# Down projection in seven products: the first two operands of each next product are fetched and split before the evictions, and product 0's first two use the weight pool

## The chip, the cores and the metric

The kernel runs on one core of a Trainium2 chip. The metric is the device time of one execution in microseconds; the number given for a kernel is the median of several executions. The core has five engines that each work through an instruction stream of their own, in order: TensorE (PE in the profile, with its weight loads as PEld), VectorE (DVE), ScalarE (ACT), GpSimd (POOL) and SyncE (SP). SyncE, GpSimd and, for a few stores, ScalarE issue the DMA transfers; an instruction that waits holds up all that stand behind it on its engine.

## The reference

Two layers over 1024 latent tokens and 256 context tokens of width 1024, all in float32: layer 0 mixes with Fourier groups and a Hyena convolution, layer 1 with neighbourhood attention. Each ends with a SwiGLU feed-forward block of width 2816. That block's last product is what the change touches:

```python
def swiglu(u, w_gate, w_up, w_down):
    return (jax.nn.silu(u @ w_gate) * (u @ w_up)) @ w_down
...
        h_lat = h_lat + g1 * y_lat
        h_lat = h_lat + g2 * swiglu(modulate(rms_norm(h_lat, norm2_g[i]), sh2, sc2),
                                    ffn_w_gate[i], ffn_w_up[i], ffn_w_down[i])
        if not last:
            ...
            h_ctx = h_ctx + cg2 * swiglu(modulate(rms_norm(h_ctx, norm2_g[i]), csh2, csc2),
                                         ffn_w_gate[i], ffn_w_up[i], ffn_w_down[i])
    return rms_norm(h_lat, final_g)
```

`h_lat` is the latent stream, `h_ctx` the context stream; the context is carried through layer 0 only.

## The kernel before

Float32 precision is built from pairs: every operand is split into a rounded high half and the rest, and a product is three matmuls (high x high, high x low, low x high). `split` (L284 to L288) does it: ScalarE casts the high half (L286), VectorE subtracts it from the source (L288). Large latent products are computed by the Strassen-Winograd scheme: seven products of half-size blocks instead of eight.

**Gate and up.** `ffn` (L1309) runs eleven blocks of gate and up. Each block's weights come through the pool `pw` (two buffers for each of the tags `ws`, `wh`, `wl`): raw weights in `ws`, their halves in `wh` and `wl` and in smaller tiles. The matmuls are at L1264; ScalarE copies a running accumulator out before TensorE goes on adding to it (`snap`, L1269). VectorE combines the hidden block (L1357 to L1363), and GpSimd stores seven combinations of it to DRAM (`bops`). Between the blocks, four sums of the down weights are formed for later and stored (`sops`).

**Down.** `down` (L1414) computes the seven products p = 0 to 6 over 1024 tokens. Each has eleven steps i (`n2`). A step takes one operand pair: `operands` (L1420) loads half a tile of weights and half a tile of hidden values on SyncE (L267) and splits the 1024 columns in one go. Its three tiles come from `S4`, the pool `p4` with 20 buffers of 4 KB a partition; the raw data has a tile of its own where the weights come straight from the input (products 0, 1 and 6, `own`), else it lies in the later low half's tile. Then `prods` (L1428) issues 4 x 3 matmuls of 128x512 (L1433), one accumulator for each of four row blocks. The two accumulator sets alternate from product to product.

After the eleven steps `evict` (L1449) adds the four accumulators, scaled, to the residual stream with one VectorE instruction each (L1454). Where a block of the output is complete, ScalarE squares it (L467) for the coming norm, VectorE adds the squares (L472), and in layer 0 ScalarE stores it. The norm itself (L485 to L517) runs in pieces: `hook(i)` (L1472) advances it at fixed steps of the products 6 and later. In the last product a few last steps are held back and done one accumulator after the other.

In layer 0 the products also carry side work: each odd step advances `todo`, which loads and sums the modulation weights (`in_ada_w`, L446 to L453). After product 6 follows the context stream: 22 steps (L1518), each with a 512 KB weight load through `ws` (or a tile of `p4`), its split into `wh` and `wl`, and 24 matmuls of 128x256 (L1536).

**What sets the order.** The program is traced in the order of the Python code, and a scheduler then orders the instructions of each engine by a simulated timeline. A load is traced where it is written but goes out as early as its buffer and its place in SyncE's order allow, so product p + 1's first operands can be loaded during product p. `follow(ins)` (L225) puts the instructions of its block behind `ins` where they run on the same engine. In this program TensorE's matmuls are held in order that way (`end`); the splits and evictions on VectorE and ScalarE are not.

Of the kernel before, what the change touches and what calls it, by code (L numbers as in the profile page):

```python
# [10 lines left out]
F32 = mybir.dt.float32  # L11
# [7 lines left out]
P = 128  # L19
# [181 lines left out]
class Builder:  # L201
# [1212 lines left out]
    def down(self, l, bops, sops, hidc, hs, h, todo, after, keep):  # L1414
        nc, a = self.nc, self.a
        w = a["down"][l]
        n2 = NFB // 2
        self.banks = 6

        def operands(asrc, bsrc, own):  # L1420
            hi, lo = self.S4(F32R), self.S4(F32R)
            f = self.S4() if own else lo.bitcast(F32)
            self.ld(f[:, :512], asrc)
            self.ld(f[:, 512:], bsrc)
            self.split(f, hi, lo)
            return hi, lo

        def prods(acc, ops, j, c0, c1, first, last):  # L1428
            hi, lo = ops
            sl = slice(j * P, (j + 1) * P)  # L1430
            xs = slice(512 + c0, 512 + c1)
            for k, (x, y) in enumerate(((hi, hi), (hi, lo), (lo, hi))):
                m = nc.tensor.matmul(acc[j][:, c0:c1], x[:, sl], y[:, xs], start=first and k == 0, stop=last and k == 2,  # L1433
                                     skip_group_check=True)
            return m.ins

        def load_h(nbs, pc):
            for nb in nbs:
                if pc < 2 or nb % 2 == 0:
                    t = self.S2()  # L1440
                    if pc < 2:
                        self.ldr(t, hs[nb][:, pc * 512:pc * 512 + 512])
                        h.put(0, nb, pc, t)
                    else:
                        for k in (0, 1):
                            self.ldr(t[:, k * 256:k * 256 + 256], hs[nb + k][:, 1024:])
                            h.put(0, nb + k, 2, t[:, k * 256:k * 256 + 256])

        def evict(acc, r, j, pc, final):  # L1449
            nb = 4 * r + j  # L1450
            n = WID[pc]
            c0 = OFF[pc] % 512 if pc > 2 else 0
            t = h.ap(0, nb, pc)
            nc.vector.scalar_tensor_tensor(t, acc[j][:, c0:c0 + n], self.ada_col(l, pc, 5, nb), t, op0=MUL, op1=ADD)  # L1454
            if final and pc < 3:
                self.square(t, nb, pc)
                if l == 0 and pc < 2:
                    self.lda(keep[nb][:, pc * 512:pc * 512 + 512], t)
            elif final and j < 3:
                x = self.TK()  # L1460
                nc.scalar.activation(x[:, :n], t, AF.Square)
                sq = self.sq[1][0][:, c0:c0 + n]
                nc.vector.tensor_tensor(sq, sq, x[:, :n], ADD)

        end = None
        sets = [[self.PP() for _ in range(4)], [self.PP(), self.PP(), self.PQ(), self.PQ()]]
        seq = (("A11", "B11", 0, 1, False), ("A12", "B21", 0, 1, True), ("S2", "T2", 0, 0, False), ("S1", "T1", 1, 0, False),
               ("S3", "T3", 1, 0, True), ("S4", "B22", 0, 0, True), ("A22", "T4", 1, 1, True))
        raw = {"A11": (0, 0), "A12": (1, 0), "A22": (1, 1)}
        done = iter(())  # L1470

        def hook(i):  # L1472
            if i in (3, 6) or i > 7 and l == 0:
                next(done, None)

        for p, (ak, bk, r, pc, final) in enumerate(seq):
            acc = sets[p % 2]
            late = []
            for i in range(n2):
                hook(i)  # L1480
                if p == 0 and i == 6:
                    load_h(range(4), 1)
                if p == 1 and i in (1, 4, 7):
                    load_h(*((range(4), 0), (range(4, 8), 0), (range(4, 8), 1))[i // 3])
                if ak in raw:
                    k, q = raw[ak]
                    src = w[2 * i + k, q]
                else:
                    src = sops[i][ak]
                ops = operands(src, bops[i][bk], ak in raw)  # L1490
                if p == 6 and i >= n2 - (4 if l else 3):
                    late.append((i, ops))
                else:
                    with self.follow(end):
                        for j in range(4):
                            m = prods(acc, ops, j, 0, 512, p in (0, 1, 3) and i == 0, i == n2 - 1)
                    end = m
                if p < 5 and i % 2 or p == 5 and i < 2:
                    next(todo, None)
            for q in (3, 4) if l == 1 and p == 6 else (pc,):  # L1500
                for j in range(4):
                    c0 = OFF.get(q, 0) % 512 if q > 2 else 0
                    for i, ops in late:
                        prods(acc, ops, j, c0, c0 + WID[q], False, i == n2 - 1)
                    evict(acc, r, j, q, final)
                    if q == 3:
                        next(done, None)
                if q > 2:
                    for _ in after(q):
                        pass  # L1510
            if p == 5:
                done = after(0)
        if l == 0:
            for _ in done:
                pass
            done = after(1)
            acc = [self.PP() for _ in range(4)]
            for kb in range(NFB):  # L1518
                hook(kb)
                if kb in (4, 8, 12, 16):  # L1520
                    load_h((kb // 2 - 2, kb // 2 - 1), 2)
                t = self.S2(F32R)
                f = t[:, 256:].bitcast(F32)
                with self.follow(self.last_ldr):
                    self.ldr(f, hidc[kb // 2][:, kb % 2])
                self.split(f, t[:, :256], t[:, 256:])
                f = self.pw.tile([P, 1024], F32, tag="ws", name=self.nm("ws")) if kb % 3 < 2 else self.S4()
                wh, wl = self.pair1()
                self.ld(f.rearrange("p (r k) -> p r k", r=2), w[kb].rearrange("r p k -> p r k"))
                self.split(f, wh, wl)  # L1530
                for nb in range(KB):

                    o = acc[nb // 2][:, nb % 2 * 256:nb % 2 * 256 + 256]
                    with self.follow(end):
                        for k, (x, c) in enumerate(((wh, 0), (wh, 256), (wl, 0))):
                            m = nc.tensor.matmul(o, x[:, nb * P:(nb + 1) * P], t[:, c:c + 256],  # L1536
                                                 start=kb == 0 and k == 0 and nb % 2 == 0,
                                                 stop=kb == NFB - 1 and k == 2, skip_group_check=True)
                    end = m.ins
            for nb in range(KB):  # L1540
                x = h.ap(0, nb, 2)
                nc.vector.scalar_tensor_tensor(x, acc[nb // 2][:, nb % 2 * 256:nb % 2 * 256 + 256],
                                               self.ada_col(0, 2, 5, nb), x, op0=MUL, op1=ADD)
                self.square(x, nb, 2)
            self.last, self.end = after(2), end
        self.banks = 8
# [630 lines left out]
```

## Time and profile before

| | |
|---|---|
| median of 3 executions | 3042.79 us (3039.41 to 3048.79) |
| profiled execution | 3045.79 us, of it span 3044.0 us |
| mean granted TensorE clock | 0.985 |
| layer 0: start of product 0 / product 1 on / context product ends | about 1377 / 1430 / 1690 us |
| layer 1: start of product 0 / products 1 to 6 | about 2788 / 2842 to 3028 us |

How to read the rows below. In the timeline a row has the start in us from the span's start, the duration, the engine, the line, the operation, `written<-read` by tile names, and the number of instructions merged; a bracket gives the idle time before it and the engine, tile and line that ended it. `ps` and `pq` are accumulators, `s` a tile of `p4` (or of the smaller pool `p2`), `ws`, `wh`, `wl` the weight pool, `d` a DRAM buffer, `g` and `tk` tiles of the hidden block. SPq is a load issued on SyncE. In the list of waits a row says who waited for whom: total us, times, longest. In the table by windows each engine has its busy time and, in brackets, its instructions; the last three columns are the granted TensorE clock, the busy share of the DMA engines, and GB/s.

### The profile page before, as it was taken

The numbers are of one execution on the slowest core, as the hardware profiler recorded it, in microseconds if no ns is written. First come the engines' busy times: TensorE is split into PE (matmuls) and PEld (weight loads), VectorE is DVE, ScalarE is ACT, GpSimd is POOL, SyncE is SP. The second block draws the span as 40 slices with busy tenths as digits, with TensorE's granted clock in tenths as the row PEclk, the third lists the DMA queues.
The fourth block names the chain that finished last, engine by engine and source line by source line (L and its number), as shares of the span: only waits on it lengthen the run. The fifth ranks groups of instructions, "written<-read, shape, count | busy, mean of one in ns | idle before, by whom it ended". The sixth has DMA issues, their size and how long they took to land.

```text
span 3044.0 us, 45809 instructions
## 1 busy us (share of the span) xinstructions
PE 2907.4 (96%) x16320; PEld 2420.9 (80%) x16320; DVE 2078.8 (68%) x3988; ACT 1392.5 (46%) x2581; POOL 461.5 (15%) x753
## 2 busy tenths in 40 slices
PE   8899999999999999999999999999899999999997
PEld 3678888798899787787778888878777788887886
DVE  5767786775677777766677437777776877664545
ACT  4663225453454333333445326777674533333433
POOL 1012012451101111212010000111111022112000
PEclk9899999999999999999999999999999999999999
DMA  7565544465555444658875334444555266435663
GB/s 255 188 203 174 175 141 158 124 203 202 213 169 199 177 178 168 215 178 325 301 249 170 132 126 118 127 134 133 173 183 186 91 233 224 172 112 178 212 194 132
DMA packets 263487, 549.88 MB, mean 181 GB/s; under 512 B 33878, under 2 KB 85784, under 8 KB 263258
## 3 DMA queue, kind: packets, MB, share of 16 engines
q1 hardware_dynamic: 209658, 381.23, 38.3%
q0 software_dynamic: 51296, 161.52, 14.6%
q10 hardware_dynamic: 2304, 4.20, 0.4%
q8 instruction: 128, 2.10, 0.3%
q14 instruction: 101, 0.83, 0.1%
HBM read 418.63 MB, written 119.80 MB: 177 GB/s over the span
## 4 chain that ended last, share of the span: by engine, by line
PE 37%; issue 16%; DVE 6%; DMA 5%; POOL 2%; ACT 1%; SPq 0%; POOLq 0%; DVEq 0%; ACTq 0%
PE ps L1264 10%; PE pq L282 8%; PE ps L282 7%; PE ps L1433 4%; PE pq L1264 3%; PE ps L1536 2%; DMA s<-d 1%; PE ps L1734 1%; PE pq L1433 1%; POOL d L273 1%; DVE s L288 1%; DMA g<-in_bias 1%; DMA ws<-in_up 1%; DMA s<-in_ada_w 1%; DMA ws<-in_gate 0%
## 5 line engine op out<-in xcount | busy, mean ns | idle before, releaser
L1264 PE MATMUL ps<-s,s 128*128 128x512 f32 x2028 | 513.0, 395 | 18.5 <-ACT g L1269 12.4
L1264 PEld LDWEIGHTS ps<-s,s 128*128 128x128 f32 x2028 | 384.6, 190 | 106.4 <-ACT g L1269 16.6
L282 PE MATMUL ps<-s,wh 128*128 128x256 f32 (+1 forms) x1768 | 393.4, 328 | 1.3 <-ACT wh L286 1.3
L282 PEld LDWEIGHTS ps<-s,wh 128*128 128x128 f32 x1768 | 293.1, 189 | 36.9 <-ACT wh L286 3.4
L286 ACT CAST wh<-ws 128x1024 fp32r<-128x1024 f32 (+1 forms) x139 | 142.5, 1025 | 362.6 <-PE ps L282 160.6
L282 PE MATMUL pq<-s,wh 128*128 128x512 f32 (+1 forms) x984 | 301.0, 385 | 4.0 <-DVE s L2009 2.8
L1433 PE MATMUL ps<-s,s 128*128 128x512 f32 (+1 forms) x1000 | 258.5, 384 | 11.2 <-DVE s L288 10.9
L288 DVE TENSOR_TENSOR wl<-ws,wh 128x1024 fp32r<-128x1024 f32 (+1 forms) x139 | 165.5, 1191 | 148.6 <-ACT wh L286 142.6
L286 ACT CAST s<-s 128x1024 fp32r<-128x1024 f32 (+2 forms) x188 | 171.8, 941 | 195.6 <-DMA s<-d 160.7
L282 PE MATMUL ps<-s,wl 128*128 128x256 f32 (+1 forms) x884 | 255.9, 327 | 0.8 <-DVE wl L288 0.8
L282 PE MATMUL ps<-s,s 128*128 128x64 f16 (+3 forms) x2663 | 216.1, 233 | 23.8 <-DVE st L1722 12.9
L1433 PEld LDWEIGHTS ps<-s,s 128*128 128x128 f32 x1000 | 183.7, 188 | 53.0 <-DVE s L288 17.1
L286 ACT CAST s<-t 128x512 fp32r<-128x512 f32 (+2 forms) x250 | 140.5, 579 | 178.0 <-DVE t L1243 74.4
L288 DVE TENSOR_TENSOR s<-s,s 128x1024 fp32r<-128x1024 f32 (+2 forms) x166 | 190.8, 1185 | 42.7 <-ACT s L286 42.2
L282 PEld LDWEIGHTS pq<-s,wh 128*128 128x128 f32 x984 | 178.3, 190 | 37.9 <-DVE s L2009 3.0
L288 DVE TENSOR_TENSOR s<-t,s 128x512 fp32r<-128x512 f32 (+2 forms) x250 | 166.1, 678 | 54.7 <-ACT s L286 29.3
L1264 PE MATMUL ps<-s,wh 128*128 128x512 f32 x608 | 192.2, 393 | 1.1 <-DVE g L1357 1.1
L282 PE MATMUL ps<-s,mat 128*128 128x512 f32 x684 | 179.5, 409 | 5.9 <-ACT s L286 3.3
L282 PE MATMUL pq<-s,wl 128*128 128x512 f32 (+1 forms) x492 | 182.6, 380 | 0.3 <-DVE wl L288 0.3
L282 PEld LDWEIGHTS ps<-s,wl 128*128 128x128 f32 x884 | 162.7, 189 | 18.2 <-DVE wl L288 1.4
L334 ACT CAST mat<-cs 128x1024 fp32r<-128x1024 f16 (+2 forms) x120 | 111.6, 935 | 129.2 <-PE ps L282 55.1
L282 PEld LDWEIGHTS ps<-s,mat 128*128 128x128 f32 x684 | 132.0, 196 | 41.8 <-DVE s L288 5.5
(380 smaller groups left out, 5667.9 us busy)
## 6 DMA issues: line engine op xcount, KB each, us to landing
s<-d SPq DMA_DIRECT2D x286, 256.0 KB, 3.6
s<-in_down SPq DMA_DIRECT2D x154, 256.0 KB, 4.3
d<-s POOLq DMA_DIRECT2D x137, 256.0 KB, 3.7
d<-tk POOLq DMA_DIRECT2D x98, 256.0 KB, 3.7
s<-in_ada_w POOLq DMA_DIRECT2D x48, 512.0 KB, 4.7
g<-in_bias SPq DMA_DIRECT2D x128, 192.0 KB, 2.9
ws<-in_up SPq DMA_DIRECT2D x44, 512.0 KB, 3.6
d<-g POOLq DMA_DIRECT2D x87, 256.0 KB, 3.2
```

The lines of the kernel that those rows point to most:

```text
L273: self.last_ldr = self.nc.gpsimd.dma_start(out, in_).ins
L282: self.nc.tensor.matmul(o, l, r, start=st, stop=sp)
L286: self.last_hi = nc.scalar.copy(hi, src).ins
L288: self.last_lo = eng.tensor_tensor(lo, src, hi.bitcast(F32), SUB).ins
L334: self.nc.scalar.copy(m, st)
L1264: nc.tensor.matmul(ps, x[:, sl], y, start=first and j == 0 and x is wh and y is xh, stop=j == 3 and x is wl, skip_group_check=True)
L1433: m = nc.tensor.matmul(acc[j][:, c0:c1], x[:, sl], y[:, xs], start=first and k == 0, stop=last and k == 2, skip_group_check=True)
L1536: m = nc.tensor.matmul(o, x[:, nb * P:(nb + 1) * P], t[:, c:c + 256], start=kb == 0 and k == 0 and nb % 2 == 0, stop=kb == NFB - 1 and k = ...
L1734: nc.tensor.transpose(ps[:, j * P:(j + 1) * P], src[:, j * P:(j + 1) * P], self.ident)
```

## The change

Three things are changed, all in `down`.

1. A new helper `fetch(p, i)` does what the loop did to get an operand. At the end of each product's steps and before its evictions, the operands 0 and 1 of the next product are fetched and split; the next product's first two steps take them from `ready`.
2. The evictions of products 0 to 5 are put behind the last split so far, on ScalarE and on VectorE (`follow(self.last_hi)`, `follow(self.last_lo)`).
3. The raw data of product 0's first two operands goes into the tag `ws` of the weight pool instead of `p4`. The context weights' loads and splits, which use the same tag, are put behind the load and the split of product 5's last operand (`mark`).

```diff
@@ operands
-            f = self.S4() if own else lo.bitcast(F32)
+            f = lo.bitcast(F32)
+            if own:
+                f = self.S4() if own == 1 else self.pw.tile([P, 1024], F32, tag="ws", name=self.nm("ws"))
             self.ld(f[:, :512], asrc)
             self.ld(f[:, 512:], bsrc)
             self.split(f, hi, lo)
@@ before the loop over the products
+        def fetch(p, i):
+            ak, bk = seq[p][:2]
+            if ak in raw:
+                k, q = raw[ak]
+                return operands(w[2 * i + k, q], bops[i][bk], 2 if p == 0 and i < 2 else 1)
+            return operands(sops[i][ak], bops[i][bk], 0)
+
+        ready, mark = [], (None, None, None)
         for p, (ak, bk, r, pc, final) in enumerate(seq):
@@ in the loop over the steps
-                if ak in raw:
-                    k, q = raw[ak]
-                    src = w[2 * i + k, q]
-                else:
-                    src = sops[i][ak]
-                ops = operands(src, bops[i][bk], ak in raw)
+                ops = ready.pop(0) if ready else fetch(p, i)
+                if p == 5 and i == n2 - 1:
+                    mark = self.last_ld, self.last_hi, self.last_lo
@@ after the steps
+            if p < 6:
+                ready = [fetch(p + 1, i) for i in (0, 1)]
             for q in (3, 4) if l == 1 and p == 6 else (pc,):
                 for j in range(4):
...
-                    evict(acc, r, j, q, final)
+                    with self.follow(self.last_hi if p < 6 else None), self.follow(self.last_lo if p < 6 else None):
+                        evict(acc, r, j, q, final)
@@ context product, step kb
-                self.ld(f.rearrange("p (r k) -> p r k", r=2), w[kb].rearrange("r p k -> p r k"))
-                self.split(f, wh, wl)
+                with self.follow(mark[0]), self.follow(mark[1]), self.follow(mark[2]):
+                    self.ld(f.rearrange("p (r k) -> p r k", r=2), w[kb].rearrange("r p k -> p r k"))
+                    self.split(f, wh, wl)
```

In the changed instruction streams the same work stands in each engine's order. On SyncE the two loads of operand 0 and of operand 1 of product 0 follow the last `in_up` load, and the first four context weights' loads stand around operand 0's loads of product 6. On ScalarE the cast of product 0's operand 1 still precedes the next `snap` copy, in both layers.

## The prediction

> **What bounds the kernel now.** I read the page first, then the waits of the two down stages, then the timeline of TensorE, VectorE, ScalarE and SyncE around each place where TensorE stood still.
>
> ```profile
> PE 2907.4 (96%) x16320; PEld 2420.9 (80%) x16320; DVE 2078.8 (68%) x3988; ACT 1392.5 (46%) x2581; POOL 461.5 (15%) x753
> ...
> 1401.21 25.85 PE ps L1433 x114
> ```
>
> TensorE is busy for 96% of the span, and the change leaves its matmuls as they are. The second row is from the chain of waits: 114 down matmuls in 25.85 us, 0.227 us apart. Only time in which TensorE stands still can go. One matmul's record lasts 0.39 us, so the idle time shown before the next is 0.16 us less than the time lost. The waits of the two stages (first layer 0, from 1370 to 1690 us, then layer 1, from 2780 us; total, times, longest):
>
> ```profile
> DVE s L1454 <- PE ps L1433: 44.3, 7, 8.8
> PE ps L1433 <- DVE s L288: 8.2, 9, 1.8
> PE ps L1264 <- ACT g L1269: 4.3, 3, 2.8
> PE ps L1536 <- DVE wl L288: 2.8, 2, 2.0
> PE ps L1433 <- ACT s L286: 1.0, 1, 1.0
> ...
> DVE s L1454 <- PE ps L1433: 83.9, 8, 14.9
> PE ps L1264 <- ACT g L1269: 3.3, 1, 3.3
> PE ps L1433 <- DVE s L288: 2.6, 2, 1.7
> ```
>
> Three kinds of stall matter: L1433 waiting for the low half of an operand (VectorE, L288), L1264 (the last gate/up products, among which product 0 begins) waiting for a ScalarE snapshot, and the context product at L1536. The first and sixth rows show the cover: VectorE stands idle 44.3 and 83.9 us in front of evictions.
>
> **Part 1: operands 0 and 1 of the next product ahead of the evictions.** A boundary in layer 0, on VectorE and TensorE:
>
> ```profile
> 1459.03 1.41 DVE L1454 SCALAR_TENSOR_TENSOR s<-ps,c,s 128x512 f32<-128x512 f32 x2 [6.41 <-PE ps L1433]
> 1460.42 1.41 DVE L1454 SCALAR_TENSOR_TENSOR s<-pq,c,s 128x512 f32<-128x512 f32 x2
> 1461.74 1.22 DVE L288 TENSOR_TENSOR s<-s,s 128x1024 fp32r<-128x1024 f32 x1
> ...
> 1463.02 2.11 PE L1433 MATMUL ps<-s,s 128*128 128x512 f32 x8 [1.76 <-DVE s L288]
> ```
>
> VectorE waits 6.41 us for the accumulators, evicts for 2.8 us, and only then makes the low half that TensorE wants. Two splits (2 x 1.2 us on VectorE, 2 x 1.05 on ScalarE, as the casts below) fit into that 6.41 us. The eviction is then up to 2.4 us later only if the splits were late. Nothing needs it soon: its accumulators are used again one product later (11 steps of 12 matmuls, 30 us). Operand 2 is wanted two steps on (24 x 0.227 = 5.4 us), after 2.8 us of evictions and one split of 1.2, so the stall does not merely move on.
>
> Of layer 0's nine waits one, of 1.61 us, is in the middle of product 6 (below). The other eight stand at the first steps after a boundary: 8.2 - 1.6 = 6.6 us, with 8 x 0.16 = 7.9 us lost. In layer 1 the 1.69 us wait is one, 1.85 us lost. Together 9.7; I take **9.0** (bounds 5 and 10: VectorE's backlog after some boundaries stays).
>
> **Part 2: the middle of product 6.** Every later split moves one place forward in the queues.
>
> ```profile
> 1599.85 3.40 DVE L514 SCALAR_TENSOR_TENSOR t<-s,c,t 128x512 f32<-128x512 f32 x5 [0.39 <-ACT t L500]
> 1603.16 2.35 DVE L288 TENSOR_TENSOR s<-s,s 128x1024 fp32r<-128x1024 f32 x2
> ...
> 1604.44 2.11 PE L1433 MATMUL ps<-s,s 128*128 128x512 f32 x8 [1.61 <-DVE s L288]
> ```
>
> The split that TensorE wanted lay behind five normalisations; in the changed program it stands before them and the next one behind, with 2.7 us more time. Layer 0 has 1.61 + 0.99 idle here (2.9 lost), layer 1 has 2.6 - 1.69 = 0.9 (1.1 lost). I take half, **2.0** (bounds 0 and 4.0).
>
> **Part 3: the start of layer 0's down.** Now the context weights' first two loads and splits stand here; after the change operands 0 and 1 take the weight buffer, and the context weights go behind product 5.
>
> ```profile
> 1371.19 1.22 DVE L288 TENSOR_TENSOR wl<-ws,wh 128x1024 fp32r<-128x1024 f32 x1
> 1372.43 0.38 SPq L267 DMA_DIRECT2D ws<-in_down  x1
> 1378.64 1.05 ACT L286 CAST wh<-ws 128x1024 fp32r<-128x1024 f32 x1 [4.75 <-DMA ws<-in_down]
> 1381.50 0.57 ACT L1269 COPY g<-ps 128x512 f32<-128x512 f32 x1
> 1382.13 7.21 PE L1264 MATMUL ps<-s,s 128*128 128x512 f32 x24 [2.83 <-ACT g L1269]
> ...
> 1388.45 1.05 ACT L286 CAST s<-s 128x1024 fp32r<-128x1024 f32 x1 [5.88 <-DMA s<-d]
> ```
>
> The snapshot TensorE needs was queued on ScalarE behind a cast waiting 6.2 us (1372.43 to 1378.64) for a context weight. In the new order operand 1's cast stands there, and its load still waits for the one buffer that VectorE frees at about 1372.4: the head-of-line wait is exchanged, not removed. Between the cast and the snapshot one cast of 1.05 us and its 0.3 us wait drop out, so with the same landing TensorE resumes 1.4 us sooner; with the page's median landing for a down load, 4.3 us, 3.3 us sooner:
>
> ```profile
> s<-in_down SPq DMA_DIRECT2D x154, 256.0 KB, 4.3
> ```
>
> Two of product 0's matmuls are moved behind the stall (0.45 us more). The other two L1264 waits (1.5 idle, 1.75 lost, one behind the 5.88 us wait) should go, since two further 512 KB loads left the queue. After the long stall TensorE also runs slow:
>
> ```profile
> 1382.10:1384.00 1.90, 1.87 (x4) 1.49 (x5) 1.90 (x6) 0.47 (x1) 0.00 (x0) 0.50 0.81 237
> 1463.00:1464.00 1.00, 0.98 (x4) 0.85 (x5) 1.00 (x3) 1.00 (x2) 0.00 (x0) 1.00 1.00 322
> 2796.00:2798.00 2.00, 2.00 (x6) 1.61 (x5) 0.00 (x0) 0.00 (x0) 0.00 (x0) 0.50 0.96 374
> ```
>
> The last but two columns show the granted clock: 0.50 after the stalls of 2.83 and 3.30 us, 1.00 after 1.76. So 24 matmuls took 7.21 instead of 5.6, 1.6 us lost. Sum for this start: 1.4 to 3.3, less 0.45, plus 1.75, plus 0 to 1.6: 2.7 to 6.2. Since ScalarE may wait for operand 1 as long as the 9.6 us of the next block (3.4 more than 6.2), the lower bound is -1; I take **3.0**.
>
> [...]
>
> **Part 4: the start of layer 1's down.**
>
> ```profile
> 2769.40 0.69 DVE L288 TENSOR_TENSOR s<-ws,s 128x512 fp32r<-128x512 f32 x1 [2.11 <-PE ps L1264]
> 2779.22 0.33 SPq L267 DMA_DIRECT2D s<-in_down  x1
> 2781.96 0.33 SPq L267 DMA_DIRECT2D s<-in_down  x1
> 2788.86 1.05 ACT L286 CAST s<-s 128x1024 fp32r<-128x1024 f32 x1 [6.65 <-DMA s<-d]
> 2792.48 1.04 ACT L286 CAST s<-s 128x1024 fp32r<-128x1024 f32 x1 [2.58 <-DMA s<-d]
> 2793.43 0.58 ACT L1269 COPY g<-ps 128x512 f32<-128x512 f32 x1
> 2794.07 4.61 PE L1264 MATMUL ps<-s,s 128*128 128x512 f32 x12 [3.30 <-ACT g L1269]
> ```
>
> Operand 1's load stood on SyncE until 2779.22 for a 20-buffer tile; it took 9.6 us to its cast, operand 2's 10.5, and the snapshot was behind both. The weight pool is free here from 2770.1 (end of the first row), so operand 1 starts 9 us sooner and operand 2 no later than now, with 512 KB less ahead of it. At stake are 3.30 + 0.16 idle and 12 matmuls in 4.61 instead of 2.9 (1.7): 5.2 us. Operand 2 still stands before the snapshot, so I take **3.5** (bounds 0 and 5.2).
>
> **Part 5: the context weights moved.** Four loads of 512 KB and two splits go from product 0 to the end of product 5.
>
> ```profile
> 1566.17 0.39 SPq L267 DMA_DIRECT2D s<-in_down  x1
> 1573.78 3.49 DVE L288 TENSOR_TENSOR s<-s,s 128x1024 fp32r<-128x1024 f32 x3
> 1586.09 1.41 DVE L1454 SCALAR_TENSOR_TENSOR s<-ps,c,s 128x512 f32<-128x512 f32 x2 [8.82 <-PE ps L1433]
> ...
> 1580.00:1585.00 5.00, 5.00 (x24) 4.14 (x23) 0.00 (x0) 0.00 (x0) 0.00 (x0) 1.00 0.00 0
> ```
>
> The loads for product 6 start at 1566.17; two context loads now precede them, two more wait on SyncE until VectorE has split the first two (behind its three last splits, until about 1579.6), and operand 1 is queued behind. The window shows every engine but TensorE, and the DMA engines, idle from 1580 to 1585, so operand 1 lands at about 1584 and is split by 1586.5; TensorE wants it at 1591 (product 5 ends about 1 us after its first eviction, 1586.09; one step of 2.7 and four high matmuls of 0.9 follow). Cost **0**, upper bound 4 (a landing 9 us long). The context product's own two waits (2.8) stay.
>
> **Sum.** 9.0 + 2.0 + 3.0 + 3.5 = 17.5 us. Against the profiled execution's 3045.8 (span 3044.0) that is 3028.3; that execution lies 3.0 above the median of 3042.8, so on the median's scale 3025.3. Some dozen gate/up instructions change order at layer 1's first block: 1 us either way. Forecast **3026**.
>
> **Rivals.**
> - *The starts stay.* Operand 1's cast blocks ScalarE as the context weight did in layer 0, and operand 2's in layer 1. For it: both still stand ahead of the snapshot. Against it: less traffic ahead. Only parts 1 and 2 less 2 us are won, 9: 3034.
> - *The stalls only move on.* After product 4 VectorE is busy for the whole 5.00 us of a window, so what isn't late at step 0 is late at step 3. Against it: of eight boundary waits only that of the next fence is beyond the second step. Gain 2: 3041.
>
> ```profile
> 1560.00:1565.00 5.00, 3.99 (x18) 3.00 (x17) 5.00 (x13) 5.00 (x12) 0.00 (x0) 1.00 0.83 302
> ...
> 1563.55 1.20 PE L1433 MATMUL ps<-s,s 128*128 128x512 f32 x4 [1.01 <-DVE s L288]
> ```
>
> - *Slower: product 6 starved.* If the four context loads take 9 us each, about what layer 1's loads in Part 4 took, operand 1 of product 6 waits behind two of them before the splits and two after: 1566 + 18 + 2.3, then 18 + 2.3 gives 1606.6 against 1591, 15.6 us. The evictions behind its split are 20 us late, and the norm's matmul, in TensorE's order in product 6, waits 5 more; both stalls drop the clock (1.6 each). 24 lost against the other parts' 14 gained: 3053. With a landing of x the stall is 4x - 20.4 us: it begins at 5.1 us a load and has eaten the other parts at 6.5. Against it: two loads issued together are in flight together, one such load took 6.2 us in product 0's heavier traffic, and the DMA engines run empty by 1580.
> - *Everything goes*: both starts, their slow clock and the middle of product 6: 10 + 4 + 6.2 + 5.2 = 25.4: 3017.
>
> **How the numbers follow.** Forecast with "everything" 0.70, starts stay 0.14, moves on 0.09, slower 0.07. No change within 0.3%, 9.1 us, is about what a measurement here can tell: 3033.7 to 3051.9. The forecast's cases and half of "the starts stay" are faster: 0.77; the other half and "moves on" the same: 0.16; slower 0.07. The range takes in "everything" less 3 us of spread between runs (3039.4 is 3.4 below the median) and reaches to the third case: 3014 to 3040.
>
> **What would show it.** Right: no wait of L1433 for L288 above 0.5 us at the first two steps of a product, with the splits inside VectorE's idle time before L1454; waits of L1264 for L1269 under 2 us at both starts and a granted clock of 1.00 after them. Wrong: a cast of an operand waiting for DMA on ScalarE just before a snapshot; waits at steps 2 to 5 in place of the old ones; a wait for L288 or L286 at product 6's second step.

## The result, and the profile after

| | before | changed |
|---|---|---|
| median, same chip | 3043.58 us (3039.41 to 3048.79, 6 executions) | 3022.79 us (3019.11 to 3029.22, 6) |
| ratio | | 0.9934, 95% interval 0.9919 to 0.9949 |
| span of the profiled execution | 3044.0 us | 3024.4 us |

The kernel became 0.66% faster, 20.8 us by the medians; the forecast was 3026. Two more runs of it gave 0.9934 (0.9920 to 0.9948) and 0.9932 (0.9915 to 0.9950).

The table by windows, first of the kernel before and then of the changed one, each row from the first down product to the first context matmul of layer 0; columns as in the prediction.

```profile
1378.00:1616.00 238.00, 224.99 (x970) 181.04 (x969) 165.41 (x287) 99.87 (x125) 40.82 (x77) 0.99 0.80 284
```

```profile
1379.00:1602.00 223.00, 219.42 (x968) 180.51 (x967) 165.85 (x286) 100.15 (x125) 39.87 (x75) 1.00 0.86 302
```

TensorE was without work for 13.0 us of this stage and is now for 3.6 (one more stall, of 1.38 us, now lies behind the first context matmul). Work and traffic are all but the same (238 us at 284 GB/s are 67.6 MB, 223 us at 302 GB/s 67.3 MB), so the DMA engines' share rises only because the stage is shorter. The waits of the changed kernel's two down stages (layer 0 until 1690 us; then layer 1 from 2765):

```profile
DVE s L1456 <- PE ps L1435: 25.8, 5, 7.5
PE ps L1435 <- ACT s L286: 3.3, 2, 1.9
PE ps L1547 <- DVE wl L288: 2.9, 2, 2.1
PE ps L1435 <- DVE s L288: 1.6, 1, 1.6
...
DVE s L1456 <- PE ps L1435: 73.9, 8, 14.7
PE ps L1435 <- DVE s L288: 1.5, 2, 0.9
PE ps L1264 <- ACT g L1269: 0.8, 1, 0.8
```

(L1435, L1456 and L1547 are the old L1433, L1454 and L1536.) Nine waits of layer 0 for VectorE's halves have become one, and no matmul of layer 0 waits for a snapshot. One row grew: the waits for ScalarE's halves, from 1.0 to 3.3 us. VectorE's idle time in front of evictions fell from 44.3 to 25.8 us: the splits now stand in it. The timeline of the boundary that the prediction's Part 1 showed, VectorE first and then TensorE:

```profile
1448.00 2.36 DVE L288 TENSOR_TENSOR s<-s,s 128x1024 fp32r<-128x1024 f32 x2
1453.89 1.41 DVE L1456 SCALAR_TENSOR_TENSOR s<-ps,c,s 128x512 f32<-128x512 f32 x2 [3.53 <-PE ps L1435]
1455.22 1.40 DVE L1456 SCALAR_TENSOR_TENSOR s<-pq,c,s 128x512 f32<-128x512 f32 x2
...
1455.05 1.07 PE L1435 MATMUL ps<-s 128*128 128x512 f32 x4
1455.96 1.98 PE L1435 MATMUL ps<-s,s 128*128 128x512 f32 x8
```

The two splits are done 3.53 us before the first eviction, and TensorE goes from the high matmuls to the others without a gap. The start of layer 0's down, ScalarE and then TensorE:

```profile
1377.56 1.57 ACT L286 CAST s<-ws 128x1024 fp32r<-128x1024 f32 x2 [5.55 <-DMA ws<-d]
1379.03 0.58 ACT L1269 COPY g<-ps 128x512 f32<-128x512 f32 x1
...
1379.55 0.39 PE L1435 MATMUL ps<-s 128*128 128x512 f32 x1
1379.78 2.90 PE L1264 MATMUL ps<-s,s 128*128 128x512 f32 x12
```

Operand 1's cast still waits 5.55 us for its load with the snapshot behind it, but the snapshot ends at 1379.61, 0.17 us before TensorE has worked through to it. Layer 1's start, in the same order:

```profile
2775.76 1.05 ACT L286 CAST s<-s 128x1024 fp32r<-128x1024 f32 x1 [6.03 <-DMA s<-d]
2776.71 0.58 ACT L1269 COPY g<-ps 128x512 f32<-128x512 f32 x1
...
2777.34 3.02 PE L1264 MATMUL ps<-s,s 128*128 128x512 f32 x12 [0.82 <-ACT g L1269]
```

Here the snapshot is late by 0.82 us instead of 3.30, and the twelve matmuls take 3.02 us instead of 4.61. In product 6 of layer 0 things got worse (VectorE, ScalarE, TensorE):

```profile
1574.55 1.23 DVE L288 TENSOR_TENSOR s<-s,s 128x1024 fp32r<-128x1024 f32 x1 [6.01 <-ACT s L286]
1588.25 3.40 DVE L514 SCALAR_TENSOR_TENSOR t<-s,c,t 128x512 f32<-128x512 f32 x5 [0.39 <-ACT t L500]
1591.57 2.35 DVE L288 TENSOR_TENSOR s<-s,s 128x1024 fp32r<-128x1024 f32 x2
...
1596.41 0.41 ACT L286 CAST s<-s 128x256 fp32r<-128x256 f32 x1 [2.64 <-DMA s<-d]
1598.17 1.35 ACT L286 CAST s<-s 128x256 fp32r<-128x256 f32 x2 [1.35 <-DMA s<-d]
1607.06 1.66 ACT L286 CAST s<-s 128x256 fp32r<-128x256 f32 x3 [4.12 <-DMA s<-d]
...
1592.85 2.11 PE L1435 MATMUL ps<-s,s 128*128 128x512 f32 x8 [1.61 <-DVE s L288]
1599.57 1.19 PE L1435 MATMUL ps<-s 128*128 128x512 f32 x4 [1.90 <-ACT s L286]
1608.46 1.20 PE L1435 MATMUL ps<-s 128*128 128x512 f32 x4 [1.38 <-ACT s L286]
```

The splits still stand behind five normalisations and are late by the same 1.61 us as before. Two more stalls follow casts on ScalarE: 128x256 halves of the context's hidden values, which wait for their transfers and hold up the operands' casts (the rows of 1.35 and 1.66 us have the operand's cast as their last one). The lost time here is 5.4 us, against 2.9 before.

### The profile page after: what moved, and what is told of

Same layout as the page of the kernel before. It is cut to its first block, busy times and chain, and to the rows that moved or that the text cites. A ratio compares the mean times of both kernels' runs of the same rounds, so it can differ in the third digit from the quotient of the medians.

```text
span 3024.4 us, 45819 instructions
## 1 busy us (share of the span) xinstructions
PE 2901.8 (96%) x16320; PEld 2420.3 (80%) x16320; DVE 2079.2 (69%) x3988; ACT 1393.9 (46%) x2581; POOL 461.2 (15%) x753
## 3 DMA queue, kind: packets, MB, share of 16 engines
q0 software_dynamic: 51296, 161.52, 14.6%
## 4 chain that ended last, share of the span: by engine, by line
PE 45%; issue 13%; DVE 4%; DMA 4%; ACT 1%; POOL 1%; POOLq 0%; DVEq 0%; ACTq 0%; SPq 0%
PE ps L1264 17%; PE pq L282 8%; PE ps L282 7%; PE ps L1435 5%; PE pq L1264 3%; PE ps L1547 2%; PE pq L1435 1%; PE ps L1745 1%; DMA g<-in_bias 1%; DMA s<-d 1%; POOL d L273 1%; DVE g L1733 0%; DMA d<-s 0%; DVE wl L288 0%; DMA d<-tk 0%
## 5 line engine op out<-in xcount | busy, mean ns | idle before, releaser
L288 DVE TENSOR_TENSOR wl<-ws,wh 128x1024 fp32r<-128x1024 f32 (+1 forms) x139 | 165.4, 1191 | 140.4 <-ACT wh L286 134.5
L1435 PE MATMUL ps<-s,s 128*128 128x512 f32 (+1 forms) x1000 | 258.6, 384 | 3.3 <-DVE s L288 3.1
L288 DVE TENSOR_TENSOR s<-s,s 128x1024 fp32r<-128x1024 f32 (+2 forms) x162 | 186.7, 1184 | 47.5 <-ACT s L286 46.8
L1435 PEld LDWEIGHTS ps<-s,s 128*128 128x128 f32 x1000 | 184.5, 188 | 41.9 <-DVE s L288 5.6
L288 DVE TENSOR_TENSOR s<-t,s 128x512 fp32r<-128x512 f32 (+2 forms) x250 | 164.5, 672 | 58.6 <-ACT s L286 30.9
```

The costliest lines, as they stand in the source:

```text
L288: self.last_lo = eng.tensor_tensor(lo, src, hi.bitcast(F32), SUB).ins
```

## Experiments

Every kernel computes what the changed one does; they differ in order and in buffers. Kernels of one set ran on one chip and share the runs of the kernel before.

| run | edit of the changed kernel | median | ratio to before (95%) |
|---|---|---|---|
| first set | before: 3047.44 | | |
| e1_no_stage | product 0's raw operands in `p4` | 3034.86 | 0.9963 (0.9950 to 0.9976) |
| e2_no_mark | context weights not held behind product 5 | 3038.69 | 0.9973 (0.9962 to 0.9984) |
| e3_no_ahead | no fetch ahead, no tie of evictions | 3042.30 | 0.9982 (0.9970 to 0.9994) |
| e4_no_follow | fetch ahead, evictions not tied | 3041.20 | 0.9978 (0.9969 to 0.9987) |
| second set | before: 3049.45 | | |
| a0_after | none | 3028.68 | 0.9934 (0.9920 to 0.9948) |
| v1_ctx_late | context splits behind product 6's operands | 3024.75 | 0.9920 (0.9907 to 0.9932) |
| v2_norm_late | norm pieces behind product 6's operands | 3029.86 | 0.9936 (0.9923 to 0.9950) |
| v3_both | both | 3022.19 | 0.9915 (0.9903 to 0.9927) |
| third set | before: 3046.17 | | |
| e5_only_ahead | neither e1's nor e2's part | 3038.35 | 0.9972 (0.9958 to 0.9986) |
| v3_again | as v3_both | 3024.18 | 0.9926 (0.9912 to 0.9939) |
| a1_after | none | 3027.37 | 0.9932 (0.9915 to 0.9950) |

**Is it the fetch or the tie that empties the boundaries?**

```diff
@@ e4_no_follow
-                    with self.follow(self.last_hi if p < 6 else None), self.follow(self.last_lo if p < 6 else None):
+                    with nullcontext():
                         evict(acc, r, j, q, final)
@@ e3_no_ahead: this too
-                ready = [fetch(p + 1, i) for i in (0, 1)]
+                ready = []
```

> No operand is fetched ahead and the evictions are not tied; staging and the context weights' place stay. My theory: the nine boundary waits come back (10.1 us), product 6's middle waits go back to what they were before the change (3.1 us less than in the changed kernel), both starts stay free: 3030. Rival: most of the gain is from the starts and what follows them, and the boundary waits only move to later steps: 3023 to 3025.

> Operands 0 and 1 are fetched ahead of the evictions in the program, but the evictions are not tied behind the splits. My theory: what counts is that the splits stand in the streams before VectorE waits for the accumulators; in layer 0 the scheduler now puts one split between the evictions at most boundaries, so 1 to 2 us come back there and layer 1 is unchanged: 3024. Rival: the tie alone carries the boundary gain: 3031.

The boundary of above in e4_no_follow, VectorE and TensorE:

```profile
1457.88 1.41 DVE L1456 SCALAR_TENSOR_TENSOR s<-ps,c,s 128x512 f32<-128x512 f32 x2 [6.44 <-PE ps L1435]
1459.28 1.40 DVE L1456 SCALAR_TENSOR_TENSOR s<-pq,c,s 128x512 f32<-128x512 f32 x2
1460.59 1.22 DVE L288 TENSOR_TENSOR s<-s,s 128x1024 fp32r<-128x1024 f32 x1
...
1461.86 2.11 PE L1435 MATMUL ps<-s,s 128*128 128x512 f32 x8 [1.75 <-DVE s L288]
```

The splits are fetched ahead in the code, and yet VectorE evicts first and TensorE waits 1.75 us, as before the change (1.76). Layer 0's waits for L288 come to 9.4 us in e4_no_follow and 9.8 in e3_no_ahead, seven each. So writing the fetch earlier does next to nothing by itself: the scheduler puts the evictions back in front. The boundaries need the tie, as e4_no_follow's rival had it; its theory, a loss of 1 to 2 us, was wrong.

One of the seven waits is new. At product 6's first step both kernels wait 2.82 us, where the kernel before waited 0.37. VectorE and TensorE in e3_no_ahead:

```profile
1584.92 1.22 DVE L288 TENSOR_TENSOR wl<-ws,wh 128x1024 fp32r<-128x1024 f32 x1
1586.72 1.22 DVE L288 TENSOR_TENSOR s<-s,s 128x1024 fp32r<-128x1024 f32 x1
...
1587.99 2.65 PE L1435 MATMUL ps<-s,s 128*128 128x512 f32 x8 [2.82 <-DVE s L288]
```

The split of a context weight, which the change moved to this place, now stands between the evictions and ahead of the operand's split; the eight matmuls behind the wait take 2.65 us, those behind e4_no_follow's 1.75 us took 2.11. With fetch and tie, product 6's first two operands are split ahead of the evictions (1567.33 and 1574.55 us in the changed kernel), and nothing waits.

**The two starts.**

```diff
@@ e1_no_stage
-                return operands(w[2 * i + k, q], bops[i][bk], 2 if p == 0 and i < 2 else 1)
+                return operands(w[2 * i + k, q], bops[i][bk], 1)
@@ e2_no_mark
-                with self.follow(mark[0]), self.follow(mark[1]), self.follow(mark[2]):
+                with nullcontext():
```

e5_only_ahead has both edits.

> Product 0's raw operands go back to tiles of the 20-buffer pool; the context weights stay behind product 5 and the early fetch stays. My theory: the parts are separate. Staging matters in layer 1 only, where operand 1's load otherwise waits for a pool tile: the 3.3 us wait of L1264 for the snapshot and the slow clock after it (1.7 us) come back, 4 to 5 us, and layer 0's start stays free because the context weights are gone from it: about 3027. Rival: staging is what freed both starts; then layer 0's 2.8 us wait and its slow clock come back too, 10 us in all: 3033.

> The context weights' loads and splits may again stand at product 0; staging and early fetch stay. My theory: their loads and casts in front of ScalarE's snapshots were layer 0's start stall; 2 to 6 us come back there (two casts now stand behind the second snapshot), product 6 is as in the changed kernel or up to 2 us better since its loads are not behind four 512 KB loads: about 3026. Rival: staging freed layer 0's start, and where the context weights go does not matter: 3023, no L1264 wait above 1 us.

> The fetch ahead and the tie of the evictions stay; product 0's raw operands and the order of the context weights are as in the kernel before. Theory (the parts add up, each worth the gaps it closes): the waits at the boundaries are gone (10 us less), the two starts keep theirs (3 to 5 us in each layer), and the ratio is 0.9965 to 0.997. Rival (the parts hang on one another, as the sum of the losses with one part undone suggests, 35 us against 21 in all): the time is 0.998 or more, and a gap that neither kernel had opens in product 0 or 1.

Layer 1's start in e1_no_stage, then layer 0's in e5_only_ahead (ScalarE, TensorE):

```profile
2783.55 1.04 ACT L286 CAST s<-s 128x1024 fp32r<-128x1024 f32 x1 [2.54 <-DMA s<-d]
2784.50 0.58 ACT L1269 COPY g<-ps 128x512 f32<-128x512 f32 x1
...
2785.13 4.60 PE L1264 MATMUL ps<-s,s 128*128 128x512 f32 x12 [2.38 <-ACT g L1269]
```

```profile
1393.54 1.04 ACT L286 CAST s<-s 128x1024 fp32r<-128x1024 f32 x1 [7.94 <-DMA s<-d]
1394.49 0.58 ACT L1269 COPY g<-ps 128x512 f32<-128x512 f32 x1
...
1395.12 4.54 PE L1264 MATMUL ps<-s,s 128*128 128x512 f32 x12 [4.23 <-ACT g L1269]
```

Both show the mechanism bare: a cast waits for a transfer, the snapshot stands behind it, TensorE behind the snapshot, and behind the stall the granted clock is low (0.63 from 2785 to 2787 us in e1_no_stage, 0.51 from 1395 to 1397 us in e5_only_ahead; 12 matmuls in 4.60 and 4.54 us, against 2.90 at the start of layer 0 in the changed kernel). In e1_no_stage layer 0's start has no gap: the weight pool's buffer matters in layer 1, the later context weights in layer 0. Without the latter a second thing goes wrong. SyncE's list of waits in e2_no_mark, 1364 to 1432 us, and the timeline of ScalarE and TensorE there:

```profile
SPq L267 <- DVE tk L1362: 11.8, 1, 11.8
```

```profile
1427.54 1.05 ACT L286 CAST s<-s 128x1024 fp32r<-128x1024 f32 x1 [18.19 <-DMA s<-d]
...
1428.64 2.07 PE L1435 MATMUL ps<-s 128*128 128x512 f32 x4 [7.49 <-ACT s L286]
```

SyncE stood 11.8 us for VectorE's L1362 with operand loads queued behind it, and a step inside product 0 lost 7.5 us, a wait that neither kernel had. In e5_only_ahead, without the staging too, that stall does not appear (SyncE's wait for L1362 is 5.2 us there); what makes the difference was not tested.

e5_only_ahead tells what fetch and tie are worth alone: 0.9972, 8.5 us of 3046. Its boundaries are empty (9.7 us by the gaps), its product 6 loses 5.5 us instead of 2.9, which leaves 7.1: within its interval. The theory's ratio was just missed, and no new gap opened in products 0 and 1, against the rival. But the starts alone (e3_no_ahead) are worth 0.0018, 5.5 us, and 8.5 + 5.5 = 14 is not the 20.1 of the whole change (0.9934). Each interval is some 4 us to either side, so the ratios alone do not show that the parts help one another. The traces show one place where they do: the new wait at product 6's start, 2.5 us longer than before the change and in e3_no_ahead with 0.5 us of slower matmuls behind it, some 3 us together, is paid only where the context weights are moved and the operands are not split ahead of the evictions. The rest of the difference stays open.

**The middle of product 6.** What stands in front of the operands was moved behind them:

```diff
@@ v1_ctx_late: the context's hidden values, blocks 16 and up
+            m6 = self.last_hi, self.last_lo
...
-                self.split(f, t[:, :256], t[:, 256:])
+                with self.follow(m6[0] if kb >= 16 else None), self.follow(m6[1] if kb >= 16 else None):
+                    self.split(f, t[:, :256], t[:, 256:])
@@ v2_norm_late: in hook(i)
-                next(done, None)
+                late = i > 7 and p == 6
+                with self.follow(self.last_hi if late else None), self.follow(self.last_lo if late else None):
+                    next(done, None)
... (p is set to 0 ahead of the loop over the products and to 7 behind it)
```

> The changed kernel once more, beside the next three on one chip. With the parts undone one at a time, the losses (8.8, 11.9, 14.6 and 13.4 us by the ratios) are larger than the gaps that came back in their profiles. Theory: part of that is the chip and the hour, so that the ratio is nearer 0.995 than 0.9934, some 3032 against 3047. Rival: the parts hang on one another (each saves more when the others stand), and the ratio is again 0.993 to 0.994, 3026 to 3029.

> The splits of the hidden values for context blocks 16 and up stand behind product 6's last operand split. Theory (ScalarE is in order: in product 6 of layer 0 the operand casts stand behind casts of 128x256 hidden values that wait 1.9 and 1.4 us for their transfers): the two gaps of 2.05 and 1.54 us go, the one of 1.78 us behind the five evictions stays, and the kernel is 3 to 4 us faster than the changed one. Rival (the operands of product 6 are late by themselves, behind the evictions): the gaps stay within 0.5 us of what they are, or move by one block, and the time stays. A loss is possible at the start of the context stage, where 16 more splits are due at once: then gaps appear behind product 6 and eat the gain.

> The pieces of the norm that blocks 8 and up of product 6 in layer 0 hand out stand behind product 6's last operand split. Theory (VectorE's operand split behind five pieces of the accumulation of squares is what the first gap of product 6 waits for): the 1.78 us go, the two gaps behind ScalarE stay at 3.6 us together, and the kernel is 1 to 2 us faster than the changed one. Rival (the split is late because its ScalarE cast is late, and the pieces merely fill the time): the gap stays at 1.5 us or more and the time stays.

> Both ties together. Theory: the middle of product 6 has no gap left of over 0.5 us in layer 0, and the kernel is 4 to 6 us faster than the changed one, near 0.9915 to 0.992 of the kernel before. Rival (what is held back is only late next): gaps of the same sum appear in the first blocks of the context stage, and the time is within 1.5 us of the changed kernel's.

TensorE's stalls in product 6 and in the context product, in the timelines of v1_ctx_late, v2_norm_late and v3_both:

```profile
1595.12 2.11 PE L1435 MATMUL ps<-s,s 128*128 128x512 f32 x8 [1.59 <-DVE s L288]
1637.46 0.50 PE L1549 MATMUL ps<-s,wh 128*128 128x256 f32 x2 [2.12 <-ACT wh L286]
1640.23 0.58 PE L1549 MATMUL ps<-s,wl 128*128 128x256 f32 x1 [2.27 <-DVE wl L288]
```

```profile
1606.31 1.19 PE L1435 MATMUL ps<-s 128*128 128x512 f32 x4 [0.34 <-ACT s L286]
1612.22 2.07 PE L1435 MATMUL ps<-s 128*128 128x512 f32 x4 [2.56 <-ACT s L286]
```

```profile
1609.76 0.51 PE L1551 MATMUL ps<-s,wh 128*128 128x256 f32 x2 [0.57 <-DVE s L1456]
1635.11 0.50 PE L1551 MATMUL ps<-s,wh 128*128 128x256 f32 x2 [1.95 <-ACT wh L286]
1638.24 0.58 PE L1551 MATMUL ps<-s,wl 128*128 128x256 f32 x1 [2.63 <-DVE wl L288]
```

Each tie takes away exactly the stall it was made for: with the context splits late, both waits for ScalarE are gone from product 6 and the one behind the normalisations stays; with the norm late, it is the other way round. That settles the causes. The time is another matter. In v2_norm_late the remaining wait is 2.56 us, with a granted clock of 0.57 and 0.50 behind it (1612.0 to 1613.5 us, and on to 1615.0; 4 matmuls in 2.07 us, against 1.19 behind the wait of 0.34), and the time is no better, against the theory's 1 to 2 us. In v1_ctx_late and v3_both the time lost in the context product grew from 3.2 us to 4.7 and 4.9, with a granted clock of 0.50 behind it (from 1640.2 to 1645.0 us in v1_ctx_late, from 1638.0 to 1642.0 in v3_both; 1.00 in the changed kernel from 1641.0 to 1642.5), and v3_both loses 1.2 us more there in two short waits behind evictions (the first row shows one). So part of the gain went there, as the rival had it; v1_ctx_late still came out 3.9 us under the changed kernel by the medians, with intervals that overlap. v3_both came out 6.5 us under the changed kernel by the medians, v3_again 3.2 us:

> Both ties of product 6 once more, beside the changed kernel on one chip. Theory: 4 to 6 us faster than the changed kernel, ratio 0.991 to 0.9925. Rival (the difference was the spread of the executions): within 2 us of it.

> The changed kernel beside the two above. Theory and rival alike: 0.993 to 0.9945 of the kernel before, as twice already; it is here for the comparison alone.

Both ties together have the lowest median in both sets. But v3_again's 3.2 us lies between its theory and its rival, and the intervals of its ratio and of the changed kernel's overlap: how much it gains is not settled. The two repeats of the changed kernel also answer a0_after's question: its ratio holds, so that the parts undone one by one did cost 8.8 (e1_no_stage) to 14.6 us (e3_no_ahead), by the ratios times 3047, more than the gaps that came back in one profile of each. All four were expected faster, at 3024 to 3030 us by their theories; their ratios times 3043.6 make 3032 to 3038. The granted clock, in the profiled executions of these four 0.983 to 0.986 and in the three of the changed kernel 0.985 to 0.987, may be a part of that; how large a part was not shown.

## Why the prediction was right, and which step of it was not

- **Part 1, 9.0 predicted: right.** All nine boundary waits are gone: 9.7 us by the prediction's own count. That the stall does not reappear at step 2 held, too. What the prediction did not see is that the fetch alone would have done next to nothing (e4_no_follow).
- **Part 2, +2.0 predicted: the sign was wrong; 3.1 us were lost** (layer 0 from 2.9 to 5.4, layer 1 from 1.1 to 1.8; in the two other profiles of the changed kernel layer 0 loses 3.7 in a0_after and 5.5 in a1_after, where behind a wait of 2.04 us the granted clock is 0.69 from 1608.0 to 1609.5 us). The step that failed is "in the changed program it stands before them and the next one behind, with 2.7 us more time". The operand split did move ahead of the five normalisations. But the norm moved as well: in TensorE's order its two matmuls stand behind 36 and 48 matmuls of product 6 now, where it was 24 and 36. The five L514 start one step later, with the next operand behind them, late by the same 1.61 us. The prediction moved the splits past a fixed chain, but the scheduler moved both. And it left out ScalarE: the casts of 128x256 that wait 1.35 to 4.12 us for transfers cost two stalls instead of one (v1_ctx_late).
- **Part 3, 3.0 predicted, 2.7 to 6.2 thought possible: 6.3.** The snapshot's wait, the two small ones and the 1.6 us of slow clock all went (1.00 is granted from 1370 to 1690 us). "The head-of-line wait is exchanged, not removed" was right: the cast still waits, until 1377.56 us. The size was too low because of the lower bound: operand 1's load was feared to take 9.6 us to its cast and took 5.3 (issued at 1372.28). So the snapshot ends 2.46 us sooner than before (1379.61 instead of 1382.07), within the 1.4 to 3.3 of the prediction, and that is just enough. One of the prediction's own signs of being wrong, an operand's cast that waits for its transfer just ahead of a snapshot, is there at both starts; it costs nothing here and 0.82 us in layer 1. In layer 0 it is a near thing: in the two other profiles of the changed kernel TensorE waits 1.66 and 0.64 us there.
- **Part 4, 3.5 predicted: 4.1** (3.46 to 0.98 lost, and 1.6 of slow clock: 0.50 was granted from 2796 to 2798 us, and 1.00 is from 2760 to 3000). In the two other profiles the wait is 1.07 and 1.44 us instead of 0.82. e1_no_stage brings 2.38 us of wait and the slow clock back (0.63 from 2785 to 2787 us), so that it is the weight pool's buffer that does it.
- **Part 5, 0 predicted: right.** Product 6's second operand was split at 1574.55, not at about 1586.5, and the evictions followed it without idle time. The rival of a starved product 6 did not occur; the context product's own waits stayed at 2.9 us. The zero holds only together with Part 1: without fetch and tie the moved context weights cost 2.5 us of waiting at product 6's start (e3_no_ahead, e4_no_follow).
- **The sum.** 9.7 - 3.1 + 6.3 + 4.1 = 17.0, against 17.5 predicted. That the total is so near is luck: Part 2's error of 5 us and Part 3's of 3 stand against one another. The spans differ by 19.6. The rest was not settled: stages of untouched code vary from profile to profile by several us (the 957 us ahead of layer 0's feed-forward block: 956.6 before, and 959.7, 956.1 and 958.0 in the three profiles of the changed kernel).

## What to carry to other kernels

Writing a fetch earlier need not move it where a scheduler orders the queue: look at the order that comes out, and tie the work that must come second. When a queue's order is changed, follow both sides of each stall, what waits and what it waits behind, since a chain that hangs on the same engine's order moves with it. On an engine that works in order, a cast that waits for a transfer holds up what stands behind it (ScalarE's 4.12 us of such waiting in product 6 left TensorE without work for 1.38); put such casts behind those whose data is already there, and look at where they are late next (v1_ctx_late).

## What the runs showed of the hardware

That the length of a stall alone does not decide the clock granted behind it was not expected. The table by windows shows it in product 6 of layer 0, first of e1_no_stage around a wait of 1.96 us, then of the changed kernel around one of 1.90; the granted clock is the last column but two:

```profile
1601.10:1604.50 3.40, 1.44 (x7) 0.90 (x6) 1.04 (x3) 1.98 (x4) 0.00 (x0) 1.00 0.50 177
1604.60:1607.90 3.30, 3.30 (x9) 2.52 (x9) 3.30 (x5) 3.09 (x5) 0.08 (x1) 0.50 0.38 115
```

```profile
1598.40:1601.70 3.30, 2.06 (x8) 1.40 (x9) 2.58 (x4) 3.30 (x6) 0.00 (x0) 1.00 0.02 9
1601.80:1605.10 3.30, 3.30 (x22) 2.91 (x21) 3.30 (x5) 1.14 (x2) 1.07 (x2) 1.00 0.74 241
```

The four matmuls behind these waits, in e1_no_stage, and a window of v1_ctx_late's context product:

```profile
1604.33 1.93 PE L1435 MATMUL ps<-s 128*128 128x512 f32 x4 [1.96 <-ACT s L286]
```

```profile
1640.20:1642.00 1.80, 1.76 (x8) 1.77 (x9) 1.80 (x3) 0.73 (x1) 0.00 (x0) 0.50 0.00 0
```

In e1_no_stage four matmuls took 1.93 us behind 1.96 us of waiting, with 0.50 granted from 1604.60 to 1607.90 us; in the changed kernel four took 1.19 us behind 1.90, with 1.00 granted from 1598.40 to 1605.10. A longer wait did not always have the low clock behind it: after 2.24 us in e2_no_mark 1.00 was granted from 1391.8 to 1394.5 us, and twelve matmuls took 3.06 us; after 2.38 us in e1_no_stage's layer 1 it was 0.63 from 2785 to 2787 us, and twelve took 4.60. In v1_ctx_late two stalls of 2.12 and 2.27 us, with two matmuls between them, were followed by 0.50 from 1640.2 to 1645.0 us; between the two, from 1637.5 to 1638.5, it was 1.00. What decides between such cases was not shown.

What the low clock costs beyond the stall can be read at layer 1's start: twelve matmuls in 4.61 us in the kernel before (0.50 granted from 2796 to 2798 us), in 3.02 us in the changed kernel (1.00 from 2775 to 2781 us), 1.6 us apart. And the same code pays it in one execution and not in another: in product 6 of layer 0, behind its last wait for a cast, the changed kernel's profile has 1.00 from 1607 to 1610 us and eight matmuls in 2.12 us (the wait was 1.38 us), a1_after's 0.69 from 1608.0 to 1609.5 us and eight in 3.38 us (2.04 us). Differences of a few us between single profiles should be read with that in mind.
